# Early identity products, a rearranged first norm and later query/key means in a one-core decoder layer

## The chip, the core and the metric

The kernel runs on one core of one Trainium2 chip. The metric is the device time of one execution in microseconds (us). TensorE (PE in the profile, PEld for its weight loads) multiplies, VectorE (DVE) and ScalarE (ACT) work element by element, GpSimd (POOL) builds constants and helps a little, SyncE (SP) issues most transfers. Each engine works through its own instructions in order.

## The reference

One layer of a decoder trunk over 512 tokens of width 1024, all in float32. The part that matters here is its beginning:

```python
u = rms_norm(x, mix_norm_g[l])
proj = u @ w_in[l]
q, k, v, cf_val, cf_gate, sc_x, sc_bg, sc_cg, gates = jnp.split(proj, SPLIT_IDX, axis=-1)
q = rms_norm(q.reshape(b, s, N_HEADS, HEAD_DIM), q_norm_g[l]).transpose(0, 2, 1, 3)
k = rms_norm(k.reshape(b, s, N_HEADS, HEAD_DIM), k_norm_g[l]).transpose(0, 2, 1, 3)
```

where `rms_norm` multiplies by `rsqrt(mean(x*x) + 1e-6)` and a gain. Three branches follow (stick-breaking attention with 8 heads of 64, a convolution of width 31 with a layer norm, a short gated convolution), gated, summed and projected onto x, and then a SwiGLU feed-forward part with its own norm.

## The kernel before

**Number format.** Each float32 operand of a product is split into a high half that TensorE multiplies in its fast 32-bit format and the low rest, and a product is three products: high by high, high by low, low by high (`mm3`, lines 89 to 96; all of them show as L90). A weight block is split by `wsplit`: ScalarE casts the high half (L81, `wh`), VectorE or for two early blocks GpSimd subtracts (L82, `wl`).

**Order of the work.** On TensorE the order is that of the program text. On the other engines a planner orders the instructions by priority and by when, by its own model of the durations, their inputs and buffers are free; `tc.high_priority(offset=...)` raises the priority, and `tc.issue_after(ins)` puts the instructions of a block behind `ins` on that instruction's engine. The program itself writes TensorE's order by a queue of generators: a `unit` multiplies one block of 128 output columns in eight steps of one `mm3` each, and `tick(n)` takes n steps from the queue. `defer(steps, fn)` calls `fn` after that many steps have been taken.

**Buffers.** A tag has a fixed number of buffers (`BUFS`): `t`, for temporaries of 128x512, has 6, the wide PSUM tag `mm` has 4, `z` 3, `o` 1. A new tile of a tag waits until the last user of an older one is done.

**The opening (lines 228 to 307).** x comes in eight pieces of 128 tokens by 512 columns, two for each of four token tiles. `transpose_rows(cols_g, ...)` turns the norm's gains by a small product with the identity through bank `o` and copies them out on VectorE (L230). For each token tile then: ScalarE squares and sums the first half (L282), VectorE the second (L283); the sums are added (L285); ScalarE takes Ln and Exp (L286 and L287) for a first reciprocal root; VectorE improves it by one Newton step (L290 to L292) and multiplies the identity by it (L294, the tile `a`, the "factor" in what follows). TensorE multiplies eight blocks of x by that diagonal (L296), which scales and turns the tile at once; each of these float32 products is two passes, 16 a tile. The squares of a tile are queued behind the Exp and the factor of the tile before (`before`). When all four tiles stand in the eight banks, ScalarE and VectorE write the halves of u with the gain (L302, L303), the splits of the first weights are queued behind the last factor (`queued_after`), and the units begin.

**Query and key norms (`head_norm`, lines 343 to 364).** When the unit of a pair of heads is done, ScalarE squares its result (L350), VectorE splits the squares into two halves (`split_to`, L81 and L82, tile `t`), ScalarE copies the result with the gain (L352). After `LAG` = 8 steps TensorE multiplies both halves by `head_mean`, and ScalarE and VectorE form the reciprocal root (`rsqrt`: L78, L262 to L265), multiply (L361) and write the attention's operands (queries L373 to L376, keys L387 and L388). The queue runs: query 0, key 0, the values (32 steps); then, between the steps of the attention, query 1, key 1, a short-convolution unit, query 2, a conformer unit, key 2, another short-convolution unit, query 3, a conformer unit, key 3 and the rest. One turn of the attention loop takes the scores of one group, three steps, the weights of the group before, four steps, and the mixing of the group before that. Head h needs pair h // 2.

Of the kernel before, what the change touches and what calls it, by code (L numbers as in the profile page):

```python
# [8 lines left out]
F32 = mybir.dt.float32  # L9
F32R = mybir.dt.float32r  # L10
AF = mybir.ActivationFunctionType
ALU = mybir.AluOpType
PSUM = bass.MemoryType.PSUM

P = 128
S = 512
D = 1024
KT = D // P
NT = S // P
NH = 8  # L20
DFF = 2816
EPS = 1e-6
# [1 line left out]
SCW = 3  # L24
BIG = 1e30
CONV_AT = (0, 25, 27, 27)
LAG = 8
PRIO = 2000
TICKS = (3, 4)
CT = 4  # L30
# [5 lines left out]
def hybrid_layer(ctx, tc, x, mix_norm_g, w_in, q_norm_g, k_norm_g, w_attn_out, conf_dw_w,  # L36
# [5 lines left out]
    nc = tc.nc  # L42
# [11 lines left out]
    cst = pool("cst", bufs=1)  # L54
# [5 lines left out]
    def alloc(tag, shape=(P, S), dt=F32):  # L60
        count[0] += 1
        where = ps if tag in ("mm", "z", "o") else odd if tag in ("c", "cf") else sb
        return where.tile(list(shape), dt, tag=tag, name=f"{tag}_{count[0]}", bufs=BUFS[tag])

    def psum(tag="mm"):
        return alloc(tag)

    def tmp(dt=F32, shape=(P, S)):
        return alloc("t", shape, dt)

    def table(ins):
        tc.stamp_issue_order_token(ins.ins, "table")

    def exp_log():
        table(nc.scalar.preload_act_table_set("natural_log_exp_and_others"))

    def act(o, i, f, **kw):
        table(nc.scalar.activation(o, i, f, **kw))  # L78
# [10 lines left out]
    def mm(o, lhsT, rhs, start, stop):  # L89
        nc.tensor.matmul(o, lhsT, rhs, start=start, stop=stop, skip_group_check=True)  # L90
# [10 lines left out]
    def defer(steps, fn):  # L101
        later.append([steps, fn])
# [74 lines left out]
    def load_x(tag):  # L177
        t = []
        for i in range(NT):
            t.append([alloc(tag) for _ in range(2)])  # L180
            for n in range(2):
                nc.sync.dma_start(t[i][n], x[i * P:(i + 1) * P, n * S:(n + 1) * S])
        return t

    def xblock(t, i, f):
        return t[i][f // 4][:, f % 4 * P:(f % 4 + 1) * P]

    with tc.high_priority(offset=1000000):
        xt = load_x("m")
# [26 lines left out]
    identr = ops.tile([P, P], F32R, name="identr")  # L216
    nc.gpsimd.tensor_copy(identr, ident_f)
    ident = identr.bitcast(F32)
# [8 lines left out]
    def transpose_rows(dst, src, n):  # L227
        pt = psum("o")
        nc.tensor.transpose(pt[:, :n], src[:n, :], ident[:n, :n])
        nc.vector.tensor_copy(dst, pt[:, :n])  # L230
# [35 lines left out]


    exp_log()
    transpose_rows(cols_g, rows_g, KT)
    uT = [(alloc("u", dt=F32R), alloc("u", dt=F32R)) for _ in range(KT)]  # L270
    pts = [psum(tag) for tag in ["mm"] * 4 + ["z"] * 3 + ["o"]]


    before = []
    with tc.high_priority(offset=1000000):
        for t in range(NT):
            st = cst.tile([P, 4], F32, name=f"st{t}")
            m, y, a = st[:, 0:1], st[:, 2:3], st[:, 3:4]
            with ExitStack() as behind:
                for ins in before:  # L280
                    behind.enter_context(tc.issue_after(ins))
                nc.scalar.activation(tmp(), xt[t][0], AF.Square, accum_out=m, scale=1.0 / 32)  # L282
                nc.vector.scalar_tensor_tensor(tmp(), xt[t][1], 1.0 / D, xt[t][1], ALU.mult,  # L283
                                               ALU.mult, accum_out=st[:, 1:2])
            nc.vector.scalar_tensor_tensor(m, m, EPS, st[:, 1:2], ALU.add, ALU.add)  # L285
            act(y, m, AF.Ln)  # L286
            last = nc.scalar.activation(y, y, AF.Exp, scale=-0.5)  # L287
            table(last)

            nc.vector.tensor_mul(a, y, y)  # L290
            nc.vector.scalar_tensor_tensor(a, a, -0.5, m, ALU.mult, ALU.mult)
            nc.vector.scalar_tensor_tensor(y, a, 1.5, y, ALU.add, ALU.mult)  # L292
            diag = alloc("a", (P, P))
            before = [last.ins, nc.vector.tensor_scalar_mul(diag, ident, y).ins]  # L294
            for f in range(KT):
                nc.tensor.matmul(pts[f][:, t * P:(t + 1) * P], xblock(xt, t, f), diag, start=True,  # L296
                                 stop=True, skip_group_check=True)
        queued_after[1] = before
        for f in range(KT):
            hi, lo = uT[f]  # L300
            g = cols_g[:, f:f + 1]
            parts = [nc.scalar.activation(hi, pts[f], AF.Copy, scale=g),  # L302
                     nc.vector.scalar_tensor_tensor(lo, pts[f], g, hi.bitcast(F32), ALU.mult,  # L303
                                                    ALU.subtract)]
            if f in (3, KT - 1):
                queued_after[2 if f == 3 else 3] = [ins.ins for ins in parts]
# [39 lines left out]
    def head_norm(g, done):  # L346
        def start(p):
# [6 lines left out]
            def mean():  # L354
# [7 lines left out]
                done(y)  # L362
            defer(LAG, mean)
        return start
# [330 lines left out]
    for n in range(2):  # L695
        t = alloc("v", (P, NT, S))
# [272 lines left out]
```

## Time and profile before

| | |
|---|---|
| Time, median of 3 runs | 837.4 us (837.03, 837.40, 838.48) |
| Profiled execution's own time | 837.62 us |
| Its span, first to last instruction | 835.9 us |
| TensorE busy | 821.9 us, 98% of the span |
| VectorE, ScalarE, GpSimd busy | 604.1, 397.0, 35.1 us |
| First product of u (L90) | at 16.74 us |
| Moved by DMA | 90.12 MB, 108 GB/s on average |

Times in the profile count from the start of the span. A row of the order of time has: start, duration, engine, line, operation, output <- inputs, sizes (output <- input), count of merged instructions, and in brackets how long the engine had been idle and for what. A row of the waits has: waiting engine and line, what it waited for, us in total, how often, the longest. A row of a stretch has: the stretch and its length, busy us (and instructions) of PE, PEld, DVE, ACT, POOL, the granted clock, the DMA share and GB/s.

### The profile page before, as it was taken

How to read it: one execution, taken by the hardware profiler on the slowest of the kernel's cores; microseconds unless marked ns; L12 is line 12 of the kernel's file. 1: busy time of each engine (PE TensorE's matmuls, PEld its weight loads, DVE VectorE, ACT ScalarE, POOL GpSimd, SP SyncE). 2: the span in 40 equal slices, each digit the busy share in tenths (PEclk: the TensorE clock that was granted, in tenths of full speed). 3: DMA queues.
4: the chain of work that ended last, by engine and by line, in shares of the span. 5: the costliest groups of instructions: out<-in, count | busy, mean ns of one | idle time of the engine just before them, and what ended most of it. 6: DMA issues, size and time to landing. Idle time of an engine off the chain costs nothing.

```text
span 835.9 us, 9695 instructions
## 1 busy us (share of the span) xinstructions
PE 821.9 (98%) x3727; PEld 681.7 (82%) x3727; DVE 604.1 (72%) x884; ACT 397.0 (47%) x587; POOL 35.1 (4%) x60
## 2 busy tenths in 40 slices
PE   6999999999999999999999999999999999999998
PEld 5888887888888888888888888888888788888876
DVE  5598789897899999784453447555679765556797
ACT  5336698887664232573342354333345323333451
POOL 3100010001100000000000120000000000000000
PEclk9999999999999999999999999999999999999999
DMA  7332214113112133133333333332236533322362
GB/s 253 105 101 84 68 51 151 51 51 102 51 51 101 51 138 110 55 114 112 128 122 129 101 101 102 100 102 89 75 117 230 192 128 101 102 88 76 126 202 101
DMA packets 71275, 90.12 MB, mean 108 GB/s; under 512 B 1920, under 2 KB 56380, under 8 KB 71228
## 3 DMA queue, kind: packets, MB, share of 16 engines
q1 hardware_dynamic: 70060, 87.39, 31.4%
q10 hardware_dynamic: 1168, 2.10, 0.7%
q8 instruction: 29, 0.48, 0.2%
q14 instruction: 18, 0.15, 0.1%
HBM read 87.39 MB, written 2.10 MB: 107 GB/s over the span
## 4 chain that ended last, share of the span: by engine, by line
PE 91%; DVE 6%; issue 1%; ACT 1%; DMA 1%; SPq 0%; DVEq 0%
PE mm L90 77%; PE z L90 11%; PE o L90 3%; DVE wl L82 2%; DMA m<-in_x_dram 1%; DVE cf L502 0%; DVE tt L877 0%; DVE tt L876 0%; ACT wh L81 0%; PE mm L705 0%; DVE tt L878 0%; DVE t L283 0%; DVE t L82 0%; DVE z L862 0%; DVE m L375 0%
## 5 line engine op out<-in xcount | busy, mean ns | idle before, releaser
L90 PE MATMUL mm<-u,wh 128*128 128x512 f32 x1536 | 474.9, 390 | 0.0
L90 PEld LDWEIGHTS mm<-u,wh 128*128 128x128 f32 x1536 | 287.4, 188 | 59.4 <-DVE u L303 0.6
L90 PE MATMUL mm<-u,wl 128*128 128x512 f32 x768 | 299.2, 390 | 0.0
L81 ACT CAST wh<-raw 128x1024 fp32r<-128x1024 f32 (+1 forms) x153 | 145.9, 953 | 274.0 <-PE mm L90 225.9
L82 DVE TENSOR_TENSOR wl<-raw,wh 128x1024 fp32r<-128x1024 f32 (+1 forms) x151 | 167.3, 1108 | 62.6 <-ACT wh L81 62.0
L90 PEld LDWEIGHTS mm<-u,wl 128*128 128x128 f32 x768 | 144.2, 188 | 30.0
L502 DVE SCALAR_TENSOR_TENSOR cf<-cf,cols_w,cf 128x512 f32<-128x512 f32 x120 | 89.9, 749 | 3.7 <-ACT cf L500 1.2
L793 DVE TENSOR_TENSOR t<-mm,cf 128x512 f32<-128x512 f32 x22 | 15.2, 691 | 59.7 <-PE mm L90 59.7
L90 PE MATMUL mm<-m,wh 128*128 128x512 f32 x128 | 39.4, 389 | 0.0
L81 ACT CAST wh<-tt 128x1024 fp32r<-128x1024 f32 x21 | 22.1, 1054 | 28.1 <-PE mm L90 11.7
L90 PE MATMUL mm<-wh,m 128*128 128x512 f32 x104 | 33.9, 390 | 0.0
L791 DVE TENSOR_TENSOR t<-mm,cf 128x512 f32<-128x512 f32 x22 | 15.1, 688 | 25.5 <-PE mm L90 25.4
L90 PE MATMUL z<-wh,m 128*128 128x512 f32 x84 | 29.6, 393 | 0.0
L90 PEld LDWEIGHTS mm<-m,wh 128*128 128x128 f32 x128 | 24.0, 188 | 4.9
L78 ACT ACTIVATE s<-s 128x384 f32<-128x384 f32 (+1 forms) x48 | 26.9, 561 | 1.2
L82 DVE TENSOR_TENSOR wl<-tt,wh 128x1024 fp32r<-128x1024 f32 x21 | 25.6, 1221 | 2.5 <-ACT wh L81 2.3
L90 PE MATMUL mm<-m,wl 128*128 128x512 f32 x64 | 24.9, 389 | 0.0
L90 PEld LDWEIGHTS mm<-wh,m 128*128 128x128 f32 x104 | 19.5, 188 | 4.0
L448 DVE SCALAR_TENSOR_TENSOR s<-z,s 128x384 f32<-128x384 f32 (+1 forms) x24 | 14.4, 598 | 11.6 <-ACT s L78 10.4
L90 PE MATMUL mm<-wl,m 128*128 128x512 f32 x52 | 20.7, 398 | 1.7 <-DVE wl L82 1.6
L78 ACT ACTIVATE t<-t 128x512 f32<-128x512 f32 x31 | 19.5, 631 | 3.7 <-DVE t L791 3.7
L558 DVE TENSOR_TENSOR t<-mm,t 128x512 f32<-128x512 f32 x16 | 10.9, 688 | 14.0 <-PE mm L90 14.0
(266 smaller groups left out, 1061.2 us busy)
## 6 DMA issues: line engine op xcount, KB each, us to landing
raw<-in_w_in_dram SPq DMA_DIRECT2D x23, 1024.0 KB
raw<-in_w_ffn_in_dram SPq DMA_DIRECT2D x22, 1024.0 KB
raw<-in_w_ffn_out_dram SPq DMA_DIRECT2D x11, 1024.0 KB
raw<-in_w_ffn_out_dram SPq DMA_DIRECT2D x11, 512.0 KB
raw<-in_w_in_dram SPq DMA_DIRECT2D x10, 512.0 KB
raw<-in_w_o_dram SPq DMA_DIRECT2D x4, 1024.0 KB
raw<-in_w_ffn_out_dram SPq DMA_DIRECT2D x11, 256.0 KB
m<-in_x_dram SPq DMA_DIRECT2D x8, 256.0 KB
```

Source lines behind the costliest of these rows:

```text
L78: table(nc.scalar.activation(o, i, f, **kw))
L81: (copy or nc.scalar.copy)(hi, src)
L82: (sub or nc.vector.tensor_sub)(lo, src, hi.bitcast(F32))
L90: nc.tensor.matmul(o, lhsT, rhs, start=start, stop=stop, skip_group_check=True)
L448: marks.append(nc.vector.scalar_tensor_tensor(t, z, 0.0, t, ALU.max, ALU.add))
L502: nc.vector.scalar_tensor_tensor(y, pad[:, n:n + S], w(n), y, ALU.mult, ALU.add)
L558: nc.vector.tensor_mul(s[0], y, s[0])
L791: nc.vector.tensor_mul(g, pg[0], rstd[0])
L793: nc.vector.tensor_mul(u, pu, rstd[0])
```

## The change

Three things are changed.

- 18 products of the identity with itself are put on TensorE ahead of the transposition of the gains. They write 128 columns of bank `o`, which nobody reads.
- The work on a token tile is cut into `squares`, `power` (adding the sums, Ln, Exp) and `factor` (Newton step, diagonal, products). All ScalarE instructions of these form one chain in the order written, and so do all VectorE instructions. The order is that of the last loop: the squares of tiles 2 and 3 now stand ahead of the Newton step of tiles 1 and 2.
- `LAG` is 10 in place of 8.

```diff
-LAG = 8
+LAG = 10
+WARM = 18
...
     exp_log()
+    early = psum("o")
+    for _ in range(WARM):
+        mm(early[:, :P], identr, identr, True, True)
     transpose_rows(cols_g, rows_g, KT)
...
+    chain = {}
+
+    def queued(engine, fn):
+        with ExitStack() as behind:
+            if engine in chain:
+                behind.enter_context(tc.issue_after(chain[engine].ins))
+            chain[engine] = fn()
+        return chain[engine]
...
+    def squares(t):
+        queued("act", lambda: nc.scalar.activation(
+            tmp(), xt[t][0], AF.Square, accum_out=sts[t][:, 0:1], scale=1.0 / 32))
+        queued("dve", lambda: nc.vector.scalar_tensor_tensor(
+            tmp(), xt[t][1], 1.0 / D, xt[t][1], ALU.mult, ALU.mult, accum_out=sts[t][:, 1:2]))
+
+    def power(t):
+        m, y = sts[t][:, 0:1], sts[t][:, 2:3]
+        queued("dve", lambda: nc.vector.scalar_tensor_tensor(m, m, EPS, sts[t][:, 1:2], ALU.add,
+                                                             ALU.add))
+        table(queued("act", lambda: nc.scalar.activation(y, m, AF.Ln)))
+        table(queued("act", lambda: nc.scalar.activation(y, y, AF.Exp, scale=-0.5)))
+
+    def factor(t):
+        m, y, a = sts[t][:, 0:1], sts[t][:, 2:3], sts[t][:, 3:4]
+        queued("dve", lambda: nc.vector.tensor_mul(a, y, y))
+        queued("dve", lambda: nc.vector.scalar_tensor_tensor(a, a, -0.5, m, ALU.mult, ALU.mult))
+        queued("dve", lambda: nc.vector.scalar_tensor_tensor(y, a, 1.5, y, ALU.add, ALU.mult))
+        queued("dve", lambda: nc.vector.tensor_scalar_mul(diags[t], ident, y))
+        for f in range(KT):
+            nc.tensor.matmul(pts[f][:, t * P:(t + 1) * P], xblock(xt, t, f), diags[t], start=True,
+                             stop=True, skip_group_check=True)
...
+        for step, t in ((squares, 0), (power, 0), (factor, 0), (squares, 1), (power, 1),
+                        (squares, 2), (factor, 1), (power, 2), (squares, 3), (factor, 2),
+                        (power, 3), (factor, 3)):
+            step(t)
+        before = [chain["act"].ins, chain["dve"].ins]
         queued_after[1] = before
```

The removed lines are the loop over the four tiles that did the same operations tile by tile, each tile's squares behind the factor of the tile before.

More of the change, by code (lines that the diff above doesn't have):

```diff
@@ L271, in hybrid_layer @@
     pts = [psum(tag) for tag in ["mm"] * 4 + ["z"] * 3 + ["o"]]
-    before = []
-    with tc.high_priority(offset=1000000):
[L276 to L297, printed above, removed]
@@ new lines, in hybrid_layer @@
+    chain = {}
[5 more added lines that the diff above has]
+        return chain[engine]
+    sts = [cst.tile([P, 4], F32, name=f"st{t}") for t in range(NT)]
+    diags = [alloc("a", (P, P)) for _ in range(NT)]
+    def squares(t):
[3 more added lines that the diff above has]
+            tmp(), xt[t][1], 1.0 / D, xt[t][1], ALU.mult, ALU.mult, accum_out=sts[t][:, 1:2]))
```

## The prediction

> **What bounds the kernel now.** I read the page first (busy time, with the chain that ended last, nearly all of it TensorE), then the list of who waited for whom with TensorE as the waiter, and then the order of time around each wait that list names.
>
> ```profile
> PE 821.9 (98%) x3727; PEld 681.7 (82%) x3727; DVE 604.1 (72%) x884; ACT 397.0 (47%) x587; POOL 35.1 (4%) x60
> PE mm L296 <- DVE a L294: 4.5, 2, 4.3
> PE mm L90 <- DVE t L82: 1.4, 2, 1.2
> ```
>
> TensorE is the bound. Only what shortens its idle time, or the opening before it runs solid, can show. Of its few waits the change can touch the opening (L294) and the two for "t <- DVE L82", the low halves of squares that the mean (head_mean) multiplies.
>
> **The opening.** These are VectorE rows, in order of time, columns start, duration, line, output:
>
> ```profile
> 7.69 0.69 DVE L283 SCALAR_TENSOR_TENSOR t<-m 128x512 f32<-128x512 f32 x1 [0.78 <-DMA m<-in_x_dram]
> 8.49 0.16 DVE L285 SCALAR_TENSOR_TENSOR st<-st 128x1 f32<-128x1 f32 x1
> 9.85 0.29 DVE L294 TENSOR_SCALAR a<-identr,st 128x128 f32<-128x128 f32 x1
> 10.85 0.16 DVE L285 SCALAR_TENSOR_TENSOR st<-st 128x1 f32<-128x1 f32 x1
> 11.51 0.16 DVE L290 TENSOR_TENSOR st<-st 128x1 f32<-128x1 f32 x1 [0.50 <-ACT st L287]
> 12.10 0.28 DVE L294 TENSOR_SCALAR a<-identr,st 128x128 f32<-128x128 f32 x1
> 14.34 0.29 DVE L294 TENSOR_SCALAR a<-identr,st 128x128 f32<-128x128 f32 x1
> ```
>
> Each token tile costs VectorE 2.25 us (from the factor at 9.85 to 12.10, again to 14.34). In it 0.50 us is idle while ScalarE takes Ln and Exp. The change puts the next tile's squares (0.69 us) into that hole, for tiles 1 and 2. Tile 0's hole is not filled (its factor still stands ahead of squares 1), nor is tile 3's. Naively that is 2 x 0.50 = 1.0 us. Two things can take it back: the arrival of x, and TensorE.
>
> Arrival: the new order wants the second half of tile 2 at 8.49 + 0.16 = 8.65; before, it was touched at 10.05.
>
> ```profile
> 2.18 5.49 DMA m<-in_x_dram
> 0.00:7.66 7.66, 0.93 (x4) 0.87 (x5) 1.62 (x7) 3.02 (x7) 1.98 (x14) 1.00 0.71 202
> 0.00:9.40 9.40, 2.67 (x12) 2.61 (x13) 2.79 (x12) 3.71 (x10) 2.93 (x19) 1.00 0.74 226
> ```
>
> The fourth of the eight 256 KB pieces landed at 2.18 + 5.49 = 7.67. By 7.66 the queue had moved 7.66 x 202 GB/s = 1.55 MB, about six pieces, and until 9.40 it had moved 9.40 x 226 = 2.12 MB, all eight. So the sixth piece lands between 7.7 and 9.4; I take 8.9, since the fourth landed two pieces behind the byte count. Squares 2 then run from 8.9, the tile-1 Newton step (11.51 to 12.10 is 0.59) from 9.59, its factor from 10.18 to 10.47: 0.33 later than the 9.85 to 10.14 of before. After it: sum 0.2, squares 3 0.69, Newton 0.59, factor 2 at 11.95 to 12.23 (before 12.10); sum 3 at 12.25, 0.66 to its Newton step (10.85 to 11.51), 0.59, factor 3 at 13.50 to 13.79, where before it ended at 14.63. VectorE gains 0.84.
>
> TensorE:
>
> ```profile
> 6.97 2.08 PE L296 MATMUL mm<-a,m 128*128 128x128 f32 x8 [4.31 <-DVE a L294]
> 8.84 1.45 PE L296 MATMUL z<-a,m 128*128 128x128 f32 x6
> 10.12 0.39 PE L296 MATMUL o<-a,m 128*128 128x128 f32 x2
> 10.35 1.06 PE L296 MATMUL mm<-a,m 128*128 128x128 f32 x8
> 11.24 0.83 PE L296 MATMUL z<-a,m 128*128 128x128 f32 x6
> 14.68 1.16 PE L296 MATMUL mm<-a,m 128*128 128x128 f32 x8 [0.20 <-DVE a L294]
> 16.74 0.73 PE L90 MATMUL mm<-u,wh 128*128 128x512 f32 x2
> ```
>
> A tile is 16 passes. In tile 1 eight passes take 11.24 - 10.35 = 0.89, so 0.111 each and 1.79 a tile. With about 0.1 for the first pass after a wait, the tiles run 10.6 to 12.4, 12.4 to 14.2 and 14.2 to 16.0: from tile 1 on TensorE has no gap left, so factor 3 at 13.8 waits for it. Before, tile 3 ran 14.78 to 16.57. So the opening gains 16.57 - 16.0, about 0.55, not 0.84.
>
> Do the others keep up?
>
> ```profile
> 14.69 1.23 DVE L82 TENSOR_TENSOR wl<-raw,wh 128x1024 fp32r<-128x1024 f32 x1
> 15.21 2.42 ACT L302 ACTIVATE u<-mm,cols_g 128x512 fp32r<-128x512 f32 x4 [0.55 <-PE mm L296]
> 15.93 2.73 DVE L303 SCALAR_TENSOR_TENSOR u<-mm,cols_g,u 128x512 fp32r<-128x512 f32 x4
> ```
>
> The low half of the first weights (L82) is queued behind the last factor, and its cast on ScalarE behind the last Exp, which moves alike; so it starts 0.84 earlier, at 13.85, and is done at 15.1. The first u (L302) started 0.43 after tile 3 began, now at about 14.65, its low half at 15.3 and not 15.93. So everything that feeds the first product of L90 moves by 0.55 to 0.6. Term: -0.55. Bounds: -1.0 (both holes, nothing binding) and +0.86 (rival two).
>
> **The 18 early products.** They are added work for TensorE, in its idle 4.31 us ahead of 6.97. Each is one pass of 128 columns, and a pass of the factor products, also 128 columns, is the nearest row: (8.84 - 6.97) / 8 = 0.234 in tile 0, 0.111 in tile 1. So 18 take 2.0 to 4.2 us; I take the slow end, since tile 0 is what follows an idle TensorE. From the identity's readiness at about 2.4 that ends at 6.6, with the small transpose of the gains behind it, ahead of 6.97: it fits. Cost nothing; without that cover each 0.1 us over would only push tile 0, which has until 10.5. What they can bring: tile 0 ran at 0.234 and 0.213 a pass (z: 1.28 / 6) until about 10.1, and tile 1 at 0.111, while the granted-clock column reads 1.00 throughout; the rows decide. With TensorE already fast, tile 0 ends near 8.9 in place of 10.4. Tile 1 can't start before 10.5 either way, so this is worth 0 to 0.1 against this execution. The copy of the gains out of the bank "o" comes later but is needed only by the last pair of tile 0 and by L302.
>
> **The means two steps later.** First a mean without a wait, then the two stalls, and the low halves they wait for:
>
> ```profile
> 60.67 0.61 PE L90 MATMUL mm<-t,head_mean 128*128 128x512 f32 x2
> 61.13 0.62 PE L90 MATMUL mm<-u,wh 128*128 128x512 f32 x2
> 66.57 0.39 PE L90 MATMUL mm<-t,head_mean 128*128 128x512 f32 x1
> 67.55 0.39 PE L90 MATMUL o<-wh,u 128*128 128x512 f32 x1
> 66.47 0.69 DVE L82 TENSOR_TENSOR t<-t,t 128x512 fp32r<-128x512 f32 x1
> 135.07 0.40 PE L90 MATMUL mm<-t,head_mean 128*128 128x512 f32 x1
> 136.97 0.63 PE L90 MATMUL mm<-u,wh 128*128 128x512 f32 x2
> 138.69 0.63 PE L90 MATMUL mm<-u,wh 128*128 128x512 f32 x2
> 135.89 0.69 DVE L82 TENSOR_TENSOR t<-t,t 128x512 fp32r<-128x512 f32 x1
> 137.47 0.56 DVE L82 TENSOR_TENSOR l<-s,l 128x384 fp32r<-128x384 f32 x1
> 140.76 0.40 PE L90 MATMUL z<-l,neg_ones 128*128 128x256 f32 x2
> ```
>
> A mean is two products, 61.13 - 60.67 = 0.46 without a wait, so a step of three is 0.69. The keys of pair 0 took 67.55 - 66.57 = 0.98, a loss of 0.52; the keys of pair 2 136.97 - 135.07 = 1.90, a loss of 1.44. Two steps later the first is asked for at 66.57 + 1.38 = 67.95, and its low half is done at 67.16. The second is asked for after one step, the mixing and scores of a head (138.69 - 136.97 - 0.69 = 1.03) and another step: 135.07 + 2.41 = 137.48; its low half is done at 136.58. Both waits vanish with 0.8 us over. Late next would be l, which the weights of the next score group multiply: ready at 138.03, asked for at 140.76 - 1.44 = 139.32 then, so it holds. On ScalarE a weight cast is queued behind that key's Ln and slips with it by half a us; its weights are read one unit later. No instruction and no DMA is added, and none changes its queue. Term: -1.96; bounds 0 and -1.96 for these waits, and a loss below.
>
> Sum, against the profiled execution's own 837.62 (span 835.9 and 1.7 around it; the median of the runs is 837.4, 0.2 lower): -0.55 - 1.96 = -2.51, so **835.1**.
>
> **Rivals.** One, slower: the six buffers of tag t. Today a query's mean comes one step ahead of the end of the key that follows it; two steps later it comes after it, when query and key hold four buffers each, eight where there are six. The query's Square (L262) needs a further buffer and may get it only after the key's mean has been multiplied. For pair 0 the 32 steps of the values lie ahead of its scores, and pairs 2 and 3 have another unit between query and key. Pair 1 is the tight one.
>
> ```profile
> 100.81 0.63 ACT L262 ACTIVATE t<-t 128x512 f32<-128x512 f32 x1
> 106.84 0.62 PE L90 MATMUL mm<-u,wh 128*128 128x512 f32 x2
> 109.14 0.62 ACT L262 ACTIVATE t<-t 128x512 f32<-128x512 f32 x1
> 113.78 0.69 DVE L376 TENSOR_TENSOR m<-t,m 64x512 fp32r<-64x512 f32 x1
> 116.08 0.68 DVE L388 TENSOR_TENSOR m<-t,m 64x512 fp32r<-64x512 f32 x1
> 123.12 0.22 PE L90 MATMUL z<-m,m 128*128 128x128 f32 x1
> ```
>
> The key's mean would follow the step at 106.84, so the query's Square moves from 100.81 to about 107.5, 6.7 later. The first key operand was ready at 116.76 and asked for at 123.12, 6.4 us of slack. If both chains still interleave they end some 2 us later and nothing shows. If the key's runs wholly behind the query's, the query ends at 107.5 + (114.47 - 100.81) = 121.2 and the key at 121.2 + (116.76 - 109.14) = 128.8, where TensorE, 1.1 us ahead by then, asks at 122.0: a stall of 6.8, giving 841.9. It decides once the key is over 5.3 us late. Against it: ScalarE and VectorE have gaps of 1 us and more there.
>
> Two, TensorE slow again in tiles 1 to 3. In the new order it idles from 7.0 + 0.1 + 1.79 = 8.9 to 10.5. If that undoes the early products, 14 passes take 3.15 us (6.97 to 10.12), the other 34 x 0.111 = 3.78, and tile 3 ends at 17.43: a loss of 0.86, total 837.62 + 0.86 - 1.96 = 836.5. For it: tile 0's rows show a slow TensorE after 4.3 us of idleness. Against it: the 0.20 us ahead of tile 3 left it fast, though that is far shorter. The Trainium skill (TensorE: Matmul & The Clock Gate, Part 1) says the clock falls back to half after at least one idle window of about 3.4 us, the windows running free of the kernel. By that rule 1.6 us is too short and the sum stays 835.1, where the slow rows taken again give 836.5; no row here shows a gap of such a length.
>
> Three, the second mean's wait stays: VectorE's order is planned anew, and if the low half, now with a later reader, slips by a weight half (1.2 us) behind others, most of 1.44 stays: 836.4.
>
> Four, more than the sum: executions other than the profiled one open slower (the three runs span 1.45 us) and the new order mends that too, (half of it, 0.7) with the whole 1.0 of the two holes: 835.1 - 0.45 - 0.7, about 834.0.
>
> **How the numbers follow.** Forecast 0.56 (834.4 to 835.7), rival one 0.09 (841.9), two 0.11 (836.5), three 0.15 (836.4), four 0.09 (834.0). Likeliest: 835.1. The range 833.7 to 837.8 reaches from rival four to rivals two and three together (836.5 + 1.3) and leaves out rival one. A measurement here tells 0.2%, 1.67 us, from no change: faster is below 835.7, the forecast and rival four less their edge, 0.62; within 0.2% rivals two, three and the mild form of one, 0.28; slower 0.10.
>
> **What would show it.** Right: squares 2 (L283's successor) directly behind the tile-1 sum; tile 3's passes with no wait for the factor; the first product of u at about 16.2; no TensorE wait for t in the head_mean products, and the mean at 67 and 136 without a gap. Wrong: a wait ahead of the first scores of head 2, passes of tiles 1 to 3 at 0.21, the low half of a key later than its mean, or new waits after 140 us where today there are none.

## The result: slower by 0.6%

| | before | changed |
|---|---|---|
| Median, us | 837.53 (4 runs) | 842.97 (4 runs, 841.73 to 843.29) |
| Profiled execution: its own time, span | 837.62, 835.9 | 843.29, 841.5 |
| First product of u on TensorE | 16.74 us | 20.03 us |

The ratio is 1.0061, with a 95% interval of 1.0045 to 1.0077. The forecast was 835.1, faster.

These are TensorE's waits in the changed kernel, from the list of who waited for whom (line numbers have moved: the products L90 are L91, the factor products L296 are L312, the copy of the gains L230 is L231):

```profile
PE o L91 <- POOL identr L218: 2.0, 1, 2.0
PE mm L91 <- DVE wl L83: 1.8, 3, 0.8
PE o L312 <- DVE cols_g L231: 1.7, 1, 1.7
PE o L91 <- DVE t L511: 1.4, 1, 1.4
PE mm L312 <- DVE a L310: 0.7, 1, 0.7
PE o L91 <- DVE a L83: 0.4, 1, 0.4
PE z L91 <- DVE l L83: 0.4, 1, 0.4
```

The wait for "t <- DVE L82", 1.4 us before, is gone, as forecast. The first row is the wait of the early products for the identity, in time that was idle before too. Four other waits are new: one for the copy of the gains, and three of the attention's. TensorE in the opening, in order of time:

```profile
1.99 4.10 PE L91 MATMUL o<-identr 128*128 128x128 f32 x18 [1.99 <-POOL identr L218]
7.12 2.08 PE L312 MATMUL mm<-a,m 128*128 128x128 f32 x8 [0.70 <-DVE a L310]
8.99 1.49 PE L312 MATMUL z<-a,m 128*128 128x128 f32 x6
12.18 0.79 PE L312 MATMUL o<-a,m 128*128 128x128 f32 x2 [1.71 <-DVE cols_g L231]
12.77 1.91 PE L312 MATMUL mm<-a,m 128*128 128x128 f32 x8
14.47 1.49 PE L312 MATMUL z<-a,m 128*128 128x128 f32 x6
16.18 1.17 PE L312 MATMUL mm<-a,m 128*128 128x128 f32 x8
18.08 1.06 PE L312 MATMUL mm<-a,m 128*128 128x128 f32 x8
20.03 0.73 PE L91 MATMUL mm<-u,wh 128*128 128x512 f32 x2
```

The early products fit into the gap as worked out (4.10 us). But tile 0 is still slow behind them (8.99 - 7.12 = 1.87 for eight passes, 0.23 each), its last pair (output in bank `o`) stands until 12.18, and tile 1 is slow as well (14.47 - 12.77 = 1.70 for eight, 0.21 each). Tile 2 becomes fast early in its first eight passes. So the wait for bank `o` (1.71 us) is about half of the 3.29 us by which the first product of u comes later than before; about the other half is tile 1, whose 16 passes take 0.21 us each where they took 0.11 (1.6 us in all). VectorE at the same time:

```profile
8.84 0.69 DVE L294 SCALAR_TENSOR_TENSOR t<-m 128x512 f32<-128x512 f32 x1 [0.36 <-DMA m<-in_x_dram]
11.70 0.29 DVE L310 TENSOR_SCALAR a<-identr,st 128x128 f32<-128x128 f32 x1
11.90 0.15 DVE L299 SCALAR_TENSOR_TENSOR st<-st 128x1 f32<-128x1 f32 x1
11.97 0.16 DVE L231 COPY cols_g<-o 128x8 f32<-128x8 f32 x1
13.14 0.29 DVE L310 TENSOR_SCALAR a<-identr,st 128x128 f32<-128x128 f32 x1
```

VectorE did what was forecast: squares 2 wait for their piece of x until 8.84 (forecast 8.9), factor 2 ends at 11.99 (forecast 12.23), factor 3 at 13.43 (forecast 13.79, before 14.63). Only the copy of the gains has moved: it stood behind the squares of tile 1, at 8.30, and now stands behind the sum of tile 3, at 11.97. Bank `o` is not free for tile 0's last pair until then.

In the attention, ScalarE's rows of the norm of query 1, TensorE's mean of key 1 between them (109.79), and the three waits:

```profile
102.40 0.68 ACT L79 ACTIVATE t<-mm,eps 128x512 f32<-128x512 f32 x1
109.79 0.61 PE L91 MATMUL mm<-t,head_mean 128*128 128x512 f32 x2
110.22 0.63 ACT L79 ACTIVATE t<-t 128x512 f32<-128x512 f32 x1 [0.67 <-PE mm L91]
111.13 0.62 ACT L263 ACTIVATE t<-t 128x512 f32<-128x512 f32 x1
113.05 0.44 PE L91 MATMUL o<-a,v 128*128 128x384 f32 x1 [0.41 <-DVE a L83]
116.51 0.33 PE L91 MATMUL z<-l,neg_ones 128*128 128x128 f32 x1 [0.40 <-DVE l L83]
128.30 0.73 PE L91 MATMUL o<-a,v 128*128 128x128 f32 x4 [1.41 <-DVE t L511]
```

The query's Ln runs at 102.40 and its Exp, the next thing to do, only at 110.22, right behind the mean of the key.

The two profiled executions differ by 5.67 us. By TensorE's products: 3.29 at the first product of u; 0.5 back at the mean of pair 0's keys; 3.0 more between 105 and 130 us; 1.4 back at the mean of pair 2's keys; 0.3 in small waits behind it. That is 4.6 at the last product. The last 1.0 lies behind the last addition, in writing the output; that stretch took 2.9, 3.2 or 3.9 us in the executions profiled here, so this part isn't laid to the change.

### The profile page after: what moved, and what is told of

It reads as the page before. It is cut to its first block, busy times and chain, and to the rows that moved or that the text cites. A ratio compares the mean times of both kernels' runs of the same rounds, so it can differ in the third digit from the quotient of the medians.

```text
span 841.5 us, 9725 instructions
## 1 busy us (share of the span) xinstructions
PE 828.1 (98%) x3745; PEld 687.4 (82%) x3745; DVE 603.9 (72%) x884; ACT 396.4 (47%) x587; POOL 35.3 (4%) x60
## 4 chain that ended last, share of the span: by engine, by line
PE 92%; DVE 5%; ACT 1%; DMA 1%; issue 1%; SPq 0%; DVEq 0%
PE mm L91 76%; PE z L91 11%; PE o L91 3%; DVE wl L83 1%; DMA m<-in_x_dram 1%; DVE tt L900 0%; DVE tt L899 0%; PE mm L312 0%; PE mm L728 0%; PE z L312 0%; DVE tt L901 0%; ACT wh L82 0%; SPq L183 0%; DVE m L411 0%; ACT s L79 0%
## 5 line engine op out<-in xcount | busy, mean ns | idle before, releaser
L91 PE MATMUL mm<-u,wh 128*128 128x512 f32 x1536 | 474.8, 390 | 0.1
L91 PEld LDWEIGHTS mm<-u,wh 128*128 128x128 f32 x1536 | 287.3, 188 | 59.6 <-DVE u L326 0.6
L91 PE MATMUL mm<-u,wl 128*128 128x512 f32 x768 | 299.2, 390 | 0.0
L82 ACT CAST wh<-raw 128x1024 fp32r<-128x1024 f32 (+1 forms) x153 | 145.9, 953 | 282.8 <-PE mm L91 233.3
L91 PEld LDWEIGHTS mm<-u,wl 128*128 128x128 f32 x768 | 144.2, 188 | 30.0
L91 PE MATMUL mm<-m,wh 128*128 128x512 f32 x128 | 39.4, 389 | 0.0
L82 ACT CAST wh<-tt 128x1024 fp32r<-128x1024 f32 x21 | 22.1, 1053 | 28.1 <-PE mm L91 11.7
L91 PE MATMUL mm<-wh,m 128*128 128x512 f32 x104 | 33.9, 390 | 0.0
L91 PE MATMUL z<-wh,m 128*128 128x512 f32 x84 | 29.6, 393 | 0.0
L91 PEld LDWEIGHTS mm<-m,wh 128*128 128x128 f32 x128 | 24.0, 188 | 4.9
L91 PE MATMUL mm<-m,wl 128*128 128x512 f32 x64 | 24.9, 389 | 0.0
L91 PEld LDWEIGHTS mm<-wh,m 128*128 128x128 f32 x104 | 19.5, 188 | 4.0
L91 PE MATMUL mm<-wl,m 128*128 128x512 f32 x52 | 20.7, 398 | 1.7 <-DVE wl L83 1.6
L581 DVE TENSOR_TENSOR t<-mm,t 128x512 f32<-128x512 f32 x16 | 10.9, 688 | 14.0 <-PE mm L91 14.0
L740 POOL TENSOR_TENSOR cf<-cf,t 128x512 f32<-128x512 f32 x7 | 9.9, 1416 | 255.3 <-ACT t L738 255.0
```

Source lines behind the costliest of these rows:

```text
L82: (copy or nc.scalar.copy)(hi, src)
L581: nc.vector.tensor_mul(s[0], y, s[0])
L740: nc.gpsimd.tensor_add(sumsq, sumsq, s)
```

## The experiments

Two theories came out of the traces. **A:** in the opening, the copy of the gains has lost its place on VectorE, and the early products don't speed TensorE up. **B:** in the attention, a query's norm stands still for want of buffers of tag `t` until the key behind it has had its mean. Each time is compared with the kernel before on the same chip, whose median was 837.5 to 837.9.

### The change without the later means

```diff
-LAG = 10
+LAG = 8
```

> The change without its third part (means after 8 steps, as before). Theory A, the copy of the gains: the early products put that copy behind the sum of tile 3 on VectorE, TensorE stands at the last pair of tile 0 (bank o) until about 12.2 us, and the first product of u comes near 20.0 us against 16.74: the opening alone costs 3.3 us, so about 840.8. The means wait as before (0.5 us at the keys of pair 0, 1.4 us at those of pair 2). Rival theory, everything from the later means: first product of u near 20 in the profile but the time made up later, total within 0.2% of 837.5.

Measured: 841.08, ratio 1.0034 (1.0022 to 1.0047). In its profile the copy comes at 12.64, tile 0's last pair at 12.85, the first product of u at 20.33, and both means wait as before. The opening alone costs over half of the loss.

### The new order alone

```diff
-LAG = 10
-WARM = 18
+LAG = 8
+WARM = 0
...
-    early = psum("o")
-    for _ in range(WARM):
-        mm(early[:, :P], identr, identr, True, True)
```

> Only the new order of squares and Newton steps; no early products, means after 8 steps. The copy of the gains stands behind the squares of tile 1 again. Theory A: no wait for bank o, tiles 1 to 3 run without a gap, first product of u at about 16.2, total 837.0 (0.55 us less than before, which a measurement here hardly tells). Rival theory, the new order itself is the harm (tile 1's factor is 0.3 us later and TensorE stands longer ahead of tile 1): first product of u after 17, total 838 or more.

Measured: 837.53, ratio 0.9998 (0.9989 to 1.0007). TensorE:

```profile
7.08 2.07 PE L309 MATMUL mm<-a,m 128*128 128x128 f32 x8 [4.53 <-DVE a L307]
10.66 1.91 PE L309 MATMUL mm<-a,m 128*128 128x128 f32 x8
12.36 1.01 PE L309 MATMUL z<-a,m 128*128 128x128 f32 x6
13.44 1.06 PE L309 MATMUL mm<-a,m 128*128 128x128 f32 x8
17.18 0.72 PE L91 MATMUL mm<-u,wh 128*128 128x512 f32 x2
```

The copy keeps its place and tiles 1 to 3 run without a gap, as forecast. But in this execution TensorE stays slow through tile 1's first eight passes, until about 12.8, where it was fast from 10.1 before; that takes back the half us and 0.4 more (17.18 against 16.74). So the order does no harm that can be measured. Its gain depends on when TensorE becomes fast: in the five profiled executions (this one and four below) with the new order, the copy in its old place and tile 0 beginning near 7.0 on a slow TensorE, the first product of u came at 15.97, 16.13, 16.40, 17.18 and 17.47.

### The early products alone

```diff
+    early = psum("o")
+    for _ in range(18):
+        mm(early[:, :P], identr, identr, True, True)
     transpose_rows(cols_g, rows_g, KT)
```

> The kernel before with nothing but the 18 early products. Theory A: they alone put the copy of the gains behind the squares of tile 3 on VectorE (about 12.9 us), TensorE stands at the last pair of tile 0 from 10.1 to 13.1, and the first product of u comes near 19.5 to 20.3: total 840.5 to 841.5. Rival theory (it takes the new order too): 837.6.

Measured: 841.87, ratio 1.0050 (1.0037 to 1.0063). TensorE, from the timeline:

```profile
12.56 0.79 PE L299 MATMUL o<-a,m 128*128 128x128 f32 x2 [2.47 <-DVE cols_g L230]
20.88 0.73 PE L90 MATMUL mm<-u,wh 128*128 128x512 f32 x2
```

The 18 products by themselves, in the old order, send the copy behind the squares of tile 3 and lose 4.2 us. Only the planner's order was changed by them: the time at which the copy's input is really there (6.4 us) would have left its old place open.

### The copy as the first instruction of VectorE's chain

```diff
-        nc.vector.tensor_copy(dst, pt[:, :n])
+        return nc.vector.tensor_copy(dst, pt[:, :n])
...
-    transpose_rows(cols_g, rows_g, KT)
+    with tc.high_priority(offset=1000000):
+        gains = transpose_rows(cols_g, rows_g, KT)
...
-    chain = {}
+    chain = {"dve": gains}
```

with the means after 8 steps.

> Early products and new order as in the change, means after 8 steps, but the copy of the gains is the first instruction of VectorE's chain. Theory A: the 2 us wait for bank o is gone. If the early products speed TensorE up, tile 0 runs at 0.11 us a pass and the first product of u comes at about 16.2, total 837.0. If they do not (tile 0 ran at 0.21 in the changed kernel), TensorE is slow until it has been busy some 3 us from tile 0 on, at about 10 us, and the first product of u still comes at 16.2 to 17.5. Rival theory, a slow clock by itself is the loss: tiles 1 and 2 still at 0.21 a pass and first product of u after 18.5, total 839.5 or more.

Measured: 839.41, ratio 1.0021 (1.0012 to 1.0031). The wait for bank `o` is gone, but the remedy was badly placed: the copy can't run before the early products and the transpose are through, and all of VectorE's chain stands behind it, so that tile 0 begins at 9.00 and the first product of u comes at 18.22. Neither of the expected times came: tiles 1 and 2 run fast, and the loss is all ahead of tile 0. Tile 0 is slow here too, though TensorE had multiplied for 4.1 us before.

### The copy behind the squares of tile 1

```diff
-        for step, t in ((squares, 0), (power, 0), (factor, 0), (squares, 1), (power, 1),
+        for step, t in ((squares, 0), (power, 0), (factor, 0), (squares, 1), (gains, 0),
+                        (products, 0), (power, 1),
...
+    def gains(t):
+        queued("dve", lambda: nc.vector.tensor_copy(cols_g, pg[:, :KT]))
+        pts.extend(psum(tag) for tag in ["mm"] * 4 + ["z"] * 3 + ["o"])
```

with early products, new order, and means after 8 steps.

> Early products and new order, means after 8 steps, the copy of the gains right behind the squares of tile 1, where it stood before. Theory A (the place of the copy is what the opening lost): no wait for bank o, first product of u at 16.2 to 17.2 us according to when TensorE becomes fast, total 837.0 to 837.8, as for the new order alone (837.5). Theory C (the early products are of use once the copy is out of the way): tile 0 at 0.11 us a pass, first product of u at 16.0, total below 837.0. Rival theory (early products do harm by themselves): total over 838.5.

Measured: 837.72, ratio 1.0000 (0.9990 to 1.0009). TensorE, from the timeline:

```profile
6.94 2.08 PE L319 MATMUL mm<-a,m 128*128 128x128 f32 x8 [0.53 <-DVE a L311]
10.44 1.06 PE L319 MATMUL mm<-a,m 128*128 128x128 f32 x8
15.97 0.73 PE L91 MATMUL mm<-u,wh 128*128 128x512 f32 x2
```

Against the change without the later means, this moves one copy and takes 841.08 to 837.72. That shows theory A's first half: the place of the copy is what the opening lost. Its second half stands too: the early products bring nothing that can be measured, and tile 0 is slow again.

### Only the means after 10 steps

```diff
-LAG = 8
+LAG = 10
```

> Only the means two steps later; the opening is that of before. Theory B, the buffers of tag t: the two waits for the low halves (2.0 us) vanish, but the query of pair 1 stands without buffers until its key's mean, and TensorE waits some 0.5, 0.4 and 1.6 us between 105 and 130 us for a low half of a, a low half of l, and the sum of a head: about 2.7 us, total near 838.3. Rival theory, those waits came from the late opening shifting VectorE's work: without it the waits are not there and the total is 835.5.

Measured: 838.81, ratio 1.0015 (1.0007 to 1.0024). TensorE and ScalarE in the attention, in order of time:

```profile
106.22 0.62 PE L90 MATMUL mm<-t,head_mean 128*128 128x512 f32 x2
106.65 0.63 ACT L78 ACTIVATE t<-t 128x512 f32<-128x512 f32 x1 [0.67 <-PE mm L90]
107.56 0.62 ACT L262 ACTIVATE t<-t 128x512 f32<-128x512 f32 x1
109.48 0.44 PE L90 MATMUL o<-a,v 128*128 128x384 f32 x1 [0.42 <-DVE a L82]
112.94 0.33 PE L90 MATMUL z<-l,neg_ones 128*128 128x128 f32 x1 [0.41 <-DVE l L82]
124.73 0.72 PE L90 MATMUL o<-a,v 128*128 128x128 f32 x4 [1.43 <-DVE t L488]
```

The same three waits with an untouched opening: they belong to the later means. The query's Square comes at 107.56; it stood at 100.81 before.

### The halves of the squares in another tag

```diff
-            q, sq, sh, sl = tmp(), tmp(), tmp(F32R), tmp(F32R)
+            q, sq, pair = tmp(), tmp(), alloc("tt", (P, 2, S), F32R)
+            sh, sl = pair[:, 0], pair[:, 1]
```

with `LAG = 10` and the opening of before.

> Means after 10 steps and the opening of before, as in lag10_only, but the two halves of the squares lie in one buffer of a tag that is idle in this part (tt, two buffers of 128x2x512), so that tag t has to give a query and the key behind it no more than six. Theory B, the buffers: the query's Exp and Square no longer wait for the key's mean, the three waits between 105 and 130 us (0.5, 0.4, 1.6 us) vanish and those of the means with them: 837.6 - 2.0 = 835.6. Rival theory, a mean that comes two steps later is by itself too late for the attention: the three waits stay and the total is about 838.8 as in lag10_only.

Measured: 836.76, ratio 0.9990 (0.9981 to 0.9999). The query's Exp and Square on ScalarE:

```profile
100.74 0.64 ACT L78 ACTIVATE t<-t 128x512 f32<-128x512 f32 x1
101.64 0.65 ACT L262 ACTIVATE t<-t 128x512 f32<-128x512 f32 x1
```

And the first row of TensorE's list of waits from 20 us on:

```profile
PE mm L90 <- DVE wl L82: 1.8, 3, 0.8
```

With buffers to spare and the means as late as in the change, the query's Exp and Square are back at 100.74 and 101.64, and from 20 us on TensorE's list of waits holds only the old one for wl. That settles theory B: the buffers, and not the two steps, made the three waits. The time fell by 1.0 and not by the 2.0 expected. In its profiled execution the last product comes 1.5 earlier than before although the opening was 0.5 later, which is the 2.0, and writing the output took 1.0 longer; whether the output's time belongs to this kernel or to the executions, the runs don't tell.

### All means after 9 steps

```diff
-LAG = 8
+LAG = 9
```

> The kernel before with all means after 9 steps. Theory B in its sharp form: what matters is whether a query's mean stands ahead of or behind the start of its key, and 9 steps already put it behind. So the waits between 105 and 130 us appear as with 10 steps (0.5, 0.4, 1.6 us; total about 838.5 to 839). Rival theory, the delay grows with the steps: half of it, and a total near 837.5.

Measured: 838.05, ratio 1.0004 (0.9995 to 1.0013). The query's Square is again behind the key's mean (106.80 against 104.97), and four waits appear between 112 and 129 us. With the restarts they put TensorE's products back by 2.5 us, where 10 steps put them back by 3.0. So one step more than before is enough to set the norm still, as theory B has it; but the cost grows with the delay, and the expected 838.5 was too high.

### Only the keys' means later

```diff
-    def head_norm(g, done):
+    def head_norm(g, done, lag=8):
...
-            defer(LAG, mean)
+            defer(lag, mean)
...
-        return head_norm(col("k_g"), done)
+        return head_norm(col("k_g"), done, 10)
```

with the new order and no early products.

> The new order without early products, and only the means of the keys after 10 steps, those of the queries after 8 as before, so that a query's mean still comes ahead of its key's squares. Theory B: both waits of the means vanish (2.0 us) and no new wait appears between 105 and 130 us; with the new order's own 0 to 0.5 us: 835.1 to 835.6. Rival theory (a later mean of a key is too late): waits ahead of the scores of heads 2, 4 or 6, total 837.5 or more.

Measured: 835.56, ratio 0.9975 (0.9965 to 0.9985). TensorE's whole list of waits:

```profile
PE mm L309 <- DVE a L307: 4.3, 1, 4.3
PE o L230 <- DMA rows_g<-in_mix_norm_g_dram: 2.3, 1, 2.3
PE mm L91 <- DVE wl L83: 1.8, 3, 0.8
```

Both waits of the means were at keys. Moving those alone takes them away and leaves each query ahead of its key, and nothing comes in their place. The same with the early products and the mended copy:

> All three parts of the change with both faults mended: early products and new order, the copy of the gains behind the squares of tile 1, and only the means of the keys after 10 steps. Theories A and B together say no wait for bank o, no wait of or for a mean, none between 105 and 130 us: 837.7 - 2.0, about 835.6, the same as keys10_order, since the 18 early products have brought nothing so far. Rival theory (the early products make the opening shorter on average): 835.0 or less.

Measured: 835.98, ratio 0.9980 (0.9971 to 0.9989): the intervals of the two overlap, so the early products are worth nothing that shows.

### Why the early products don't help

A constant block in place of the identity (`mm(early[:, :P], ones, ones, True, True)`, 1.25 everywhere), with the copy behind the squares of tile 1 and the means after 8 steps:

> As pin_mid, but the 18 early products multiply a constant block without zeros (1.25 everywhere) instead of the identity. If the identity's zeros are why the early products did not speed TensorE up: tile 0 at 0.11 us a pass, first product of u at 16.0, total 837.0 or less. If the data do not matter: as pin_mid, tile 0 at 0.21.

Measured: 837.82, ratio 1.0003 (0.9994 to 1.0012); tile 0 slow. The zeros are not the reason.

Then 32 of the identity instead of 18:

> As keys10_mid with 32 early products instead of 18. At the 0.217 us of the first 18 they end near 8.9 us and tile 0 follows them without a pause. If products of the identity do wake TensorE and 4.1 us of them were only too few: passes at 0.11 us from 9 us at the latest, tile 0 done before 10.5, first product of u at 16.0, total 835.2. If such products do not count at all: tile 0 slow from 8.9 on for 3 to 4 us, first product of u at 17.5 to 18, total 837.

Measured: 837.18, ratio 0.9998 (0.9989 to 1.0007). TensorE, from the timeline:

```profile
1.99 7.09 PE L91 MATMUL o<-identr 128*128 128x128 f32 x32 [1.99 <-POOL identr L218]
9.34 2.08 PE L319 MATMUL mm<-a,m 128*128 128x128 f32 x8
12.52 1.06 PE L319 MATMUL mm<-a,m 128*128 128x128 f32 x8
```

After 7 us of products almost without a pause tile 0 is still slow, and fast only from about 12.1, 2.7 us into the tile's own products. The early products are of the one-pass 32-bit format; the tile's are plain float32, two passes each. The next run changes the format alone, and one more the data too:

```diff
-        mm(early[:, :P], identr, identr, True, True)
+        mm(early[:, :P], ident, ident, True, True)
```

> keys10_mid with the early products in plain float32: 16 products of the identity, two passes each as in the products of the token tiles, 32 passes from about 2 us. If the format is what matters, passes at 0.11 us before these 32 are over (by 8.8 us). If the data matter (an identity, the same each time), slow to the end and tile 0 slow for 3 to 4 us more, first product of u near 18.

TensorE again:

```profile
1.99 5.46 PE L91 MATMUL o<-identr 128*128 128x128 f32 x32 [1.99 <-POOL identr L218]
7.66 1.16 PE L319 MATMUL mm<-a,m 128*128 128x128 f32 x8
9.88 1.16 PE L319 MATMUL mm<-a,m 128*128 128x128 f32 x8 [0.17 <-DVE a L311]
15.51 0.74 PE L91 MATMUL mm<-u,wh 128*128 128x512 f32 x2
```

A single execution took 834.45 us. The same number of passes of the same identity takes 5.46 instead of 7.09 us, since they become fast at 5.4, and tile 0 runs at 0.12 us a pass.

> As early_f32, but the 16 products multiply blocks of the first piece of x by themselves; they start when it lands (3.4 us). If the data matter: passes become fast 3 to 5 us after their start, between 6.5 and 8.5 us, tile 0 runs at 0.11 throughout and the first product of u comes near 16 to 17. If neither format nor data matter, slow as with the identity, tile 0 slow too, first product of u after 18.

A single execution took 835.74 us. Blocks of x, from 3.42 on, become fast at 7.1. So for early products of 128 columns the format decides, and the data don't show. The runs with float32 were on two other chips than the experiments with one-pass products; on the chip of the latter the float32 products of tile 0 did become fast.

The same kernel in several executions, with 16 and with 12 such products:

> The kernel of early_f32 timed in rounds. If its 834.45 was no accident of one execution: 834.3 to 835.0, below keys10_order (835.6) and keys10_mid (836.0) by the 0.5 to 1.0 us that a fast tile 0 and tile 1 save. If it was: 835.6 to 836.0.

> As f32_16 with 12 products, 24 passes: 15 slow ones until about 5.3 us and 9 fast ones end near 6.4, before tile 0's factor is ready at about 6.9, where the 32 passes end at 7.5. Tile 1 waits for VectorE either way, so the same time as f32_16 within 0.3 us; if TensorE is not yet fast when the products end in some executions, up to 0.5 us more.

Measured: 835.04 for both, ratios 0.9968 (0.9956 to 0.9980) and 0.9969 (0.9958 to 0.9979). With 16 that is at the upper end of what was expected, and with 12 it is the same, as expected. Fast passes began at 7.5 and 6.1 us in the two profiles, later than the 5.4 of the single execution. These two have the lowest medians here, 2.8 us under the kernel before on their chip: the three parts of the change with the copy kept in place, the early products in plain float32, and only the keys' means later. Their intervals still overlap with those of the same kernel with the 18 one-pass products (0.9980) and of the one with no early products (0.9975), so that float32 products pay is not shown.

**When TensorE becomes fast.** The trace of each run also holds a record of the clock granted to TensorE. Its first entry, at full speed, begins where the passes become fast: at 10.12 us before, 16.41 in the changed kernel, 12.74 with the new order alone, 12.08 behind the 32 one-pass products, 5.43, 7.47 and 6.12 behind float32 ones. Ahead of it the trace has no entry, and there the views read 1.00 while passes take 0.21 us; so a 1.00 ahead of the first entry says nothing of the clock. In the five executions named under the new order it begins at 10.34, 10.78, 10.86, 12.74 and 13.14, in the order of their first products of u (15.97 to 17.47). The full-speed entries last whole multiples of 3.413 us: 241 or 242 of them, and a single one in the change without the later means, where the clock fell again. Its stretches are:

```profile
10.14:13.55 3.41, 0.93 (x8) 0.73 (x8) 2.73 (x17) 1.88 (x9) 1.63 (x6) 1.00 1.12 357
13.55:16.97 3.42, 3.42 (x19) 3.42 (x18) 1.70 (x4) 0.58 (x1) 0.00 (x0) 0.50 1.07 371
16.97:20.00 3.03, 3.03 (x29) 3.03 (x29) 0.48 (x1) 1.20 (x3) 0.00 (x0) 1.00 0.36 124
```

In the first of them TensorE stood 2.48 us for the copy, and in the second its clock was half. So there the late copy cost its wait and slow passes behind it.

## Why the prediction was wrong, step by step

**The new order: right in its mechanism.** Squares 2 at 8.84 against 8.9, factor 3 at 13.43 against 13.79, and no gap for TensorE between tiles 1 and 3 once the copy was in place. That squares 2 came within 0.1 is partly luck: in other executions with the new order they began between 8.40 and 9.51. The first product of u, forecast at 16.2, came at 15.97 to 16.40 where TensorE was fast by 10.9, and at 17.18 and 17.47 where it was slow until 12.7 and 13.1; with the opening of before four executions gave 16.45 to 17.26. So the term of -0.55 holds for an execution in which tile 1 is fast, and the forecast took TensorE to be fast from 10 us on. Over many executions the new order alone measured nothing (0.9998); that the slow openings among them are why is likely but not shown. The range given to the term (-1.0 to +0.86) held that.

**The early products: the step that failed.** "Cost nothing", and of the copy of the gains that it "comes later but is needed only by the last pair of tile 0 and by L302". The copy's readers were named, its queue was not: VectorE's order is the planner's, the copy is not part of the chain, and its place was never costed. It cost about 3 us (841.08 against 837.72 with only the copy moved; the ratios differ by 2.8 us), and the last pair of tile 0, dismissed there, holds all of TensorE behind it, because TensorE works in order; behind the wait its passes were slow.

**"With TensorE already fast, tile 0 ends near 8.9": wrong.** It was slow behind one-pass products in every run. Rival two forecast a slow tile 1 for another reason, the pause between the tiles. In the changed kernel tile 1 was slow, but with tile 0 no faster there was no speed to be lost in the pause. Where there was, the one such trace shows it lost: without the later means the clock fell to half behind a pause of 2.48 us, while the 1.04 us ahead of tile 1 in the kernel with 12 float32 products left its passes at 0.11 us. The Trainium skill (TensorE: Matmul & The Clock Gate, Part 1) has the clock go to full after one busy window of about 3.4 us, and the windows run free of the kernel. By an estimate from that page, full clock comes 3.4 to 6.8 us after work begins. The 3.4, 4.1 and 5.5 us behind the first float32 pass agree with it, and so do the entries of 3.413 us; 7.1 us of one-pass products, longer than two such windows, do not, and there the measurement decides. The forecast took from the same part that the clock falls after an idle window of about 3.4 us; here 2.48 us without work were enough, and again the measurement decides.

**The later means: -1.96 was right, and what they cost elsewhere was the second step that failed.** The two waits vanished in every run with 10 steps for the keys (keys alone, with the new order: 835.56 against 837.53 for the new order alone, 2.0 us less). Rival one had the mechanism, the six buffers of tag t, down to the query's Square "to about 107.5" (107.56 measured with only the means moved). It failed in the sentence "If both chains still interleave they end some 2 us later and nothing shows". They did interleave, and the keys were in time; what was late were low halves of the attention's own steps and a head's sum, which share VectorE, ScalarE and tag t with the crowded norm: 3.0 us. That the buffers are behind all three is shown; by which of these ways each came late isn't. The forecast looked only at the reader of the late result, not at the neighbours in the queue. With 0.09 the rival was also given too little: eight buffers wanted where there are six was certain from the code, and only its price was open.

**Rivals three and four did not occur:** the second mean's low half was in time, and the new order alone gained nothing over many executions.

## What to carry to other kernels

An instruction added on one engine can move another one on an engine whose order is planned: after such a change, look up the place of each instruction that shares its bank or its result, and pin those that an in-order engine waits for. Where a step is delayed past the start of its neighbour, count the buffers that both hold at once; when the waits sit at one kind of caller only, as with the keys here, delay that kind alone. To warm an engine up, check in the rows behind the added work that it did become fast.

## What the runs showed of the hardware that was not expected

Early one-pass 32-bit products of 128 columns ran at 0.213 us each from the second on and left TensorE slow after 4.1 us (18 products, identity or constant) and after 7.1 us (32). Plain float32 products of the same identity became fast 3.4 to 5.5 us after their start in three profiles, and blocks of x after 3.6 us. Full clock that had been granted at 10.14 us was at half again from 13.55, behind a pause of 2.48 us, and full from 16.97. Why the two formats differ isn't shown; later in the kernel TensorE stays fast on one-pass products of 512 columns.
